# Half of the conditioning tiles of the second layer multiplied on POOL and summed by ACT instead of on DVE

## The chip, the cores and the metric

The kernel runs on one core of a Trainium2 chip. The metric is the device time of one execution in microseconds (us). One execution was also profiled, and all durations, waits and clocks below come from that one.

Engine names are those of the profile: PE is the matrix engine (PEld its weight loads), DVE the vector engine, ACT the scalar engine, POOL the GpSimd engine, SP the engine that only issues DMAs here. Each engine works through its own queue of instructions in order.

## What is computed

A trunk of two layers over 256 tokens of width 2048, all in float32. Each layer has a token mixer (an mLSTM in layer 0, softmax attention with forget gates, called FoX here, in layer 1) and a SwiGLU feed-forward network of inner width 5632. Both are wrapped in a normalisation that is modulated by six vectors, and these six vectors come from a conditioning vector `c`:

```
cs = jax.nn.silu(c)
for layer in range(DEPTH):
    mod = cs @ ada_w[layer] + ada_b[layer]
    sh1, sc1, g1, sh2, sc2, g2 = [m[:, None, :] for m in jnp.split(mod, 6, axis=-1)]
    h = rms_norm(x, norm_mix_w[layer]) * (1.0 + sc1) + sh1
    ...
    x = x + g1 * y
    h = rms_norm(x, norm_ffn_w[layer]) * (1.0 + sc2) + sh2
    x = x + g2 * swiglu(h, ffn_w_gate_up[layer], ffn_w_down[layer])
return rms_norm(x, final_norm_w)
```

The product `cs @ ada_w[layer]` is what the change is about: 2048 x 12288 weights per layer, for one row. It is a matrix-vector product, and nearly all of its cost is reading the matrix once.

## The kernel before, in words

**The large products.** Every large weight matrix is read in tiles of 4 x 128 rows by 512 columns (1 MB, `fetch`, L252 to L255) into a ring of five buffers, the pool `rawp`. To keep float32 accuracy on PE, each tile is split into a rounded high part and a rest (`split`, L257 to L265), two blocks of 128 rows at a time: ACT casts the high part `hi` (L263), and DVE subtracts it from the raw tile to get the low part `lo` (L264). Both go to a ring of four buffers (`splitp`). PE then makes three products for each block of 128 rows and each half of the tokens: L290, L291 and L292 in `mm_t`, where L291 uses `lo`. In `group_b`, used for the queries and keys of layer 1, the roles are exchanged and the products are L273 and L276. `group_a` and `group_b` loop over the rows of a matrix, four blocks of 128 at a time, and call `tick` after each.

**The conditioning.** The matrix `ada_w` is laid out so that one tile holds 128 output columns on the partitions and all 2048 inputs along the free axis. There are 96 such tiles of 1 MB per layer: six vectors (SH1, SC1, G1, SH2, SC2, G2) of 16 tiles. `ada_tile` (L191 to L198) takes a buffer from the same ring `rawp` as the weight tiles, issues the DMA on SP (L194), and lets DVE multiply the tile by the broadcast `cs` and sum along the free axis in one instruction (L195); the sum goes to one column of `acc`. After every fourth tile of a vector, `set_mods` (L177 to L189) turns four columns of `acc` into four columns of the finished vector, on DVE.

**What sets the order.** The conditioning tiles are background work. `want` puts tiles on a list, and `tick` calls `bg` with a rate: 0.75, 0.7, 0.8 and 0.5 tiles for each step of four row blocks in the four parts of the feed-forward network of layer 0, 0.66 in the FoX mixer, 0.3 in the last feed-forward network. The vectors SC1, SH1 and G1 of layer 1 are on the list from the middle of the feed-forward network of layer 0, SC2, SH2 and G2 of layer 1 from the start of the FoX mixer. Within these lists the tile framework's own scheduler orders each engine's queue, by the order of the program and by when it thinks an instruction is ready. The exception is the start of the kernel and the `bridge` (L527 to L590), the passage from one product to the next across a normalisation, where PE, DVE and ACT are listed by hand: a residual add on DVE (L429, L430), a sum of squares on ACT (L435), a reciprocal root (L454, L457), transposes on PE (L485), the affine part on ACT (L495) and on DVE (L497), the split (L510), and the first products of the next matrix (L552 to L556).

**POOL.** It holds little: constants at the start, a few memsets (L650, L633, L1202), and the DMAs of `grow` (L404, L412), which turn a finished gate vector into a row.

Of the kernel before, what the change touches and what calls it, by code (L numbers as in the profile page):

```python
# [12 lines left out]
AF = mybir.ActivationFunctionType  # L13
ALU = mybir.AluOpType
# [17 lines left out]
def kernel(  # L32
# [5 lines left out]
    nc = tc.nc  # L38
# [13 lines left out]
    def nm(s):  # L52
        n_name[0] += 1
        return f"{s}_{n_name[0]}"

    def slot(dt=F32):
        return slots.tile([P, 1024], dt, tag="slot", name=nm("slot"))
# [51 lines left out]
    acc = [const.tile([P, 96], F32, name=f"acc{i}") for i in range(2)]  # L109
# [15 lines left out]
    cs = const.tile([P, D], F32, name="cs")  # L125
# [41 lines left out]
    SH1, SC1, G1, SH2, SC2, G2 = range(6)  # L167
# [23 lines left out]
    def ada_tile(layer, vec, k):  # L191
        j = 16 * vec + k
        raw = rawp.tile([P, D], F32, tag="raw", name=nm("ada"))
        nc.sync.dma_start(raw, ada_w[layer, j])  # L194
        nc.vector.scalar_tensor_tensor(  # L195
            out=raw, in0=raw, scalar=1.0, in1=cs, op0=ALU.mult, op1=ALU.mult,
            accum_out=acc[layer][:, j : j + 1],
        )  # L198
# [17 lines left out]
    def bg(n):  # L216
        credit[0] += n
        while credit[0] >= 1.0 and background:
            credit[0] -= 1.0
            layer, v, k = background.pop(0)  # L220
            ada_tile(layer, v, k)
            if k % 4 == 3:
                set_mods(layer, v, k - 3, 4)
                done.add((layer, v, k // 4))
                if v in (G1, G2) and all((layer, v, q) in done for q in range(4)):
                    pending.append((layer, v))
        credit[0] = min(credit[0], 1.0)
# [516 lines left out]
    def early():  # L744
        for k in range(KT):
            for vec in (SC1, SH1):
                ada_tile(0, vec, k)
                if k == 0 and vec == SC1:
                    row_scale()
                set_mods(0, vec, k, 1)  # L750
                if vec == SC1:
                    yield
            if k < 4:
                norm_full(k)
            else:
                norm_tile(k, 0, SC1, SH1)
            at[0] = k + 1
            yield
# [17 lines left out]
    for k in range(4):  # L776
        upto(k + 1)
        for i in range(0, FIRST, 2):
            raw = slot()
# [209 lines left out]
    def keep_t(c0, bgn, scale=None, adv=1, layer_w=0):  # L989
        if layer_w == 0:  # L990
            i = COLS.index(c0)
            unit(i, start[i], KT, bgn)
            sp = SP[i]
            o = slot().rearrange("p (k t) -> p k t", t=T)

            def flip():
                for i in range(2):
                    nc.scalar.copy(o[:, 2 * i : 2 * i + 2, :], turned(sp, i))

            steps.append(flip)  # L1000
            return o
        o = slot().rearrange("p (k t) -> p k t", t=T)
        group_b(w, KT, c0, h_act, lambda m, ps: total(ps, o[:, m, :], scale), bgn, adv)
        return o
# [7 lines left out]
    for i in range(2):  # L1012
        q = keep_t(512 * i, LR[1 + i])
        k = keep_t(1024 + 512 * i, LR[1 + i])
# [193 lines left out]
    for i in range(4):  # L1208
# [5 lines left out]
        k = keep_t(D + 512 * i, FR, layer_w=1)  # L1214
# [123 lines left out]
```

## Time and profile before

| | us |
|---|---|
| median of two runs | 2300.57 (2300.23 to 2300.9) |
| the profiled execution, its own time | 2300.83 |
| its span, from first to last instruction | 2299.0 |
| ACT busy | 1122.8 |
| DMA queue q1, packets' time as a share of 16 engines | 74.3% |

The span is the time between the first and the last instruction of the core in the profiled execution; 1.8 us of the execution's own time lie outside it. An engine's busy time is the union of its instructions. In the view of groups, a row gives line, engine, operation, output and inputs with their shapes, the count, the busy time, the mean of one in ns, and after the second bar the idle time of that engine just before these instructions with what ended it. In the view of waits, a row gives who waited for whom, the total in us, how many times, and the longest. In the timeline, a row gives start, duration, engine, line and operation, with the idle time before it in brackets.

The layer-1 tiles that the change touches run in two stretches of the span: SC1, SH1 and G1 between 655 and 1003 us, SC2 and SH2 between 1151 and 1447 us. Between these two there is no conditioning work.

### The profile page before, as it was taken

The page shows a single profiled execution, that of the slowest core. Times are in us where ns is not written, and L with a number is a line of the kernel's source. Part 1 is how long each engine was busy: PE and PEld are TensorE (multiplying, and loading weights), DVE is VectorE, ACT ScalarE, POOL GpSimd, SP SyncE. Part 2 cuts the span into 40 slices and gives each one's busy share as a digit, 9 for nine tenths or more (in the row PEclk, how much of TensorE's full clock was granted, in tenths as well). Part 3 has the DMA queues.
Part 4 walks back from the last instruction along what each step waited for, and adds up shares of the span by engine and source line. Part 5 has one row for each costly group of instructions (what it writes and reads, how often), then busy time and mean ns, then how long its engine had stood idle before and what let it go on. Part 6 is the DMA issues. An engine that isn't in the chain of part 4 may idle for free.

```text
span 2299.0 us, 26543 instructions
## 1 busy us (share of the span) xinstructions
PE 2275.4 (99%) x10376; PEld 1861.0 (81%) x10376; DVE 1612.9 (70%) x1829; ACT 1122.8 (49%) x1488; POOL 15.6 (1%) x40
## 2 busy tenths in 40 slices
PE   8999999999999999999999999999999999999998
PEld 4777878888888888888878888888888888888886
DVE  5998788878887878865687777777655554544554
ACT  3778664555543344444555444455444433444443
POOL 0000000000000000000000000000000000000000
PEclk9999999999999999999999999999999999999999
DMA  9998989798989889985667878775766555555552
GB/s 348 364 368 320 355 313 362 271 345 325 331 331 336 323 337 337 342 293 188 215 243 285 300 259 288 255 275 186 250 241 222 191 191 198 189 187 195 193 196 105
DMA packets 89090, 623.92 MB, mean 271 GB/s; under 512 B 10034, under 2 KB 10482, under 8 KB 14596
## 3 DMA queue, kind: packets, MB, share of 16 engines
q1 hardware_dynamic: 87552, 617.79, 74.3%
q0 software_dynamic: 1264, 4.29, 0.5%
q8 instruction: 81, 1.33, 0.2%
q14 instruction: 45, 0.37, 0.0%
q10 hardware_dynamic: 148, 0.14, 0.0%
HBM read 620.05 MB, written 2.13 MB: 271 GB/s over the span
## 4 chain that ended last, share of the span: by engine, by line
PE 88%; DVE 6%; DMA 3%; ACT 2%; issue 1%; SPq 0%; ACTq 0%; DVEq 0%
PE mm L292 25%; PE mm L291 25%; PE mm L290 25%; PE mm L273 5%; DVE ada L195 3%; PE mm L276 2%; DVE lo L264 2%; DMA ada<-in_ada_w_dram 2%; PE aux L347 1%; ACT hi L263 1%; DMA raw<-in_w_in_dram 1%; DMA slot<-in_w_in_dram 1%; PE aux L945 0%; PE aux L485 0%; PE aux L1144 0%
## 5 line engine op out<-in xcount | busy, mean ns | idle before, releaser
L264 DVE TENSOR_TENSOR lo<-raw,hi 128x1024 fp32r<-128x1024 f32 x764 | 926.9, 1223 | 556.8 <-ACT hi L263 556.2
L263 ACT CAST hi<-raw 128x1024 fp32r<-128x1024 f32 x764 | 797.1, 1053 | 920.3 <-PE mm L292 816.9
L291 PE MATMUL mm<-lo,hT 128*128 128x512 f32 x1840 | 718.3, 390 | 5.3 <-DVE lo L264 5.3
L290 PE MATMUL mm<-hi,hT 128*128 128x512 f32 x1840 | 719.3, 393 | 0.0
L292 PE MATMUL mm<-hi,hT 128*128 128x512 f32 x1840 | 718.1, 390 | 0.0
L195 DVE SCALAR_TENSOR_TENSOR ada<-ada,cs 128x2048 f32<-128x2048 f32 x192 | 438.9, 2286 | 49.2 <-DMA ada<-in_ada_w_dram 49.2
L291 PEld LDWEIGHTS mm<-lo,hT 128*128 128x128 f32 x1840 | 345.7, 188 | 80.1 <-DVE lo L264 10.2
L292 PEld LDWEIGHTS mm<-hi,hT 128*128 128x128 f32 x1840 | 345.4, 188 | 72.7 <-issue 0.5
L290 PEld LDWEIGHTS mm<-hi,hT 128*128 128x128 f32 x1840 | 345.3, 188 | 70.9 <-ACT hi L263 0.5
L290 PE MATMUL mm<-hi,slot 128*128 128x512 f32 x960 | 375.1, 391 | 0.2 <-ACT slot L978 0.2
L291 PE MATMUL mm<-lo,slot 128*128 128x512 f32 x960 | 374.4, 390 | 0.0
L292 PE MATMUL mm<-hi,slot 128*128 128x512 f32 x960 | 374.4, 391 | 0.0
L290 PEld LDWEIGHTS mm<-hi,slot 128*128 128x128 f32 x960 | 180.3, 188 | 37.7 <-ACT slot L978 0.8
L292 PEld LDWEIGHTS mm<-hi,slot 128*128 128x128 f32 x960 | 180.2, 188 | 37.6 <-issue 0.7
L291 PEld LDWEIGHTS mm<-lo,slot 128*128 128x128 f32 x960 | 180.2, 188 | 37.0
L273 PE MATMUL mm<-hT,hi 128*128 128x512 f32 x512 | 181.7, 402 | 0.6 <-DVE slot L359 0.6
L276 PE MATMUL mm<-hT,lo 128*128 128x256 f32 x512 | 138.3, 280 | 0.0
L273 PEld LDWEIGHTS mm<-hT,hi 128*128 128x128 f32 x512 | 94.4, 188 | 20.5 <-DVE slot L359 0.9
L276 PEld LDWEIGHTS mm<-hT,lo 128*128 128x128 f32 x512 | 96.6, 189 | 3.0
L800 ACT ACTIVATE slot<-mm 128x512 f32<-128x512 f32 x78 | 45.0, 593 | 33.9 <-PE mm L292 31.1
L435 ACT ACTIVATE t<-X 128x512 f32<-128x512 f32 x32 | 20.2, 631 | 39.2 <-DVE X L430 39.2
L1085 ACT ACTIVATE slot<-mm 128x512 f32<-128x512 f32 x44 | 25.4, 598 | 15.0 <-PE mm L292 13.8
(207 smaller groups left out, 980.5 us busy)
## 6 DMA issues: line engine op xcount, KB each, us to landing
ada<-in_ada_w_dram SPq DMA_DIRECT2D x192, 1024.0 KB, 6.5
raw<-in_gate_up_dram SPq DMA_DIRECT2D x176, 1024.0 KB, 4.9
raw<-in_down_dram SPq DMA_DIRECT2D x88, 1024.0 KB, 4.9
raw<-in_fox_in_dram SPq DMA_DIRECT2D x48, 1024.0 KB, 5.0
raw<-in_w_in_dram SPq DMA_DIRECT2D x44, 1024.0 KB, 7.3
raw<-in_w_out_dram SPq DMA_DIRECT2D x16, 1024.0 KB, 5.8
raw<-in_fox_out_dram SPq DMA_DIRECT2D x16, 1024.0 KB, 4.9
slot<-in_w_in_dram SPq DMA_DIRECT2D x16, 256.0 KB, 12.1
```

The lines of the kernel that those rows point to most:

```text
L195: nc.vector.scalar_tensor_tensor(out=raw, in0=raw, scalar=1.0, in1=cs, op0=ALU.mult, op1=ALU.mult, accum_out=acc[layer][:, j : j + 1],)
L263: nc.scalar.copy(hi, raw[:, j : j + 2, :])
L264: nc.vector.tensor_tensor(lo, raw[:, j : j + 2, :], hi.bitcast(F32), op=ALU.subtract)
L273: nc.tensor.matmul(ps, hi, rhs, start=first, stop=last, skip_group_check=True)
L276: nc.tensor.matmul(ps[:, T:], lo, rhs[:, :T], start=False, stop=False, skip_group_check=True)
L290: nc.tensor.matmul(ps, a, hi, start=first, stop=False, skip_group_check=True)
L291: nc.tensor.matmul(ps, a, lo, start=False, stop=False, skip_group_check=True)
L292: nc.tensor.matmul(ps, b, hi, start=False, stop=last, skip_group_check=True)
L347: nc.tensor.transpose(ps[:, j * T + t * P : j * T + (t + 1) * P], src[:, t, (2 * i + j) * P : (2 * i + j + 1) * P], ident,)
L435: nc.scalar.activation(t512(), X[:, t, 512 * i : 512 * (i + 1)], AF.Square, accum_out=self.ss[:, t, i : i + 1],)
L800: nc.scalar.activation(SP[i][:, t, :], banks[t], func)
L1085: nc.scalar.activation(sg[:, t, :], banks[t], AF.Silu)
```

## The change

Of the tiles of layer 1, those with an even index `k` in all vectors but G2 leave DVE. That is 5 vectors x 8 tiles, 40 of the 192 tiles. For each, POOL multiplies the tile by `cs` in place, and ACT then passes over the product with a copy that sums along the free axis into the same column of `acc`. The other tiles, and what follows from `acc`, stay as they are.

```diff
@@ -192,6 +192,10 @@
         j = 16 * vec + k
         raw = rawp.tile([P, D], F32, tag="raw", name=nm("ada"))
         nc.sync.dma_start(raw, ada_w[layer, j])
+        if layer == 1 and vec != G2 and k % 2 == 0:
+            nc.gpsimd.tensor_tensor(raw, raw, cs, op=ALU.mult)
+            nc.scalar.activation(raw, raw, AF.Copy, accum_out=acc[layer][:, j : j + 1])
+            return
         nc.vector.scalar_tensor_tensor(
             out=raw, in0=raw, scalar=1.0, in1=cs, op0=ALU.mult, op1=ALU.mult,
             accum_out=acc[layer][:, j : j + 1],
```

## The prediction, made before the change was run

> **What bounds the kernel now.** I read the page first, for the engines' shares of the span.
>
> ```profile
> span 2299.0 us, 26543 instructions
> ...
> PE 2275.4 (99%) x10376; PEld 1861.0 (81%) x10376; DVE 1612.9 (70%) x1829; ACT 1122.8 (49%) x1488; POOL 15.6 (1%) x40
> ```
>
> PE is busy for all but 23.6 us. DVE, which the change relieves, is busy 70%. A share says little about the stretches that are touched, so the next view is the windows, cut where the touched tiles run: all engines first, then line L195 alone (instructions in brackets; each tile is two, the multiply and the read of its sum).
>
> ```profile
> 655.00:1003.00 348.00, 347.52 (x1554) 287.47 (x1553) 278.25 (x273) 143.34 (x147) 1.58 (x3) 1.00 0.90 335
> ...
> 1151.00:1447.00 296.00, 294.43 (x1575) 249.20 (x1574) 227.42 (x318) 145.29 (x239) 2.23 (x3) 1.00 0.77 276
> ```
>
> ```profile
> 655.00:1003.00 348.00, 110.11 (x96) 1.00 0.90 335
> ...
> 1151.00:1447.00 296.00, 73.51 (x64) 1.00 0.77 276
> ```
>
> The columns are PE, PEld, DVE, ACT, POOL, clock, DMA share and GB/s. In the first stretch 48 tiles run, 24 of which move; in the second 32, of which 16 move. PE is idle 0.48 us in the first and 1.57 us in the second, at full clock. DVE has 70 us and 69 us to spare, ACT more than half, POOL is empty. What PE waited for between 655 and 1447 us is the third view:
>
> ```profile
> PE mm L556 <- DVE hT L510: 0.9, 1, 0.9
> PE mm L273 <- DVE slot L359: 0.6, 1, 0.6
> PE aux L347 <- DVE slot L1088: 0.5, 1, 0.5
> ```
>
> Three waits, 2.0 us in all, none for a weight tile. So the stretches are bound by PE, and work taken off DVE can return at most 2.0 us. The question is what the new route can do to PE's supply.
>
> **How far ahead of PE the supply is.** The timeline of ACT, DVE and SP around 945 us shows the beat.
>
> ```profile
> 945.74 1.06 ACT L263 CAST hi<-raw 128x1024 fp32r<-128x1024 f32 x1 [1.67 <-PE mm L292]
> 948.46 1.05 ACT L263 CAST hi<-raw 128x1024 fp32r<-128x1024 f32 x1 [1.66 <-PE mm L292]
> 951.18 1.06 ACT L263 CAST hi<-raw 128x1024 fp32r<-128x1024 f32 x1 [1.67 <-PE mm L292]
> ...
> 956.62 1.06 ACT L263 CAST hi<-raw 128x1024 fp32r<-128x1024 f32 x1 [1.67 <-PE mm L292]
> ```
>
> ```profile
> 945.25 2.28 DVE L195 SCALAR_TENSOR_TENSOR ada<-ada,cs 128x2048 f32<-128x2048 f32 x1
> 947.46 0.08 DVE L195 DVE_READ_ACCUMULATOR ada<-ada,cs 128x1 f32 x1
> 947.46 1.22 DVE L264 TENSOR_TENSOR lo<-raw,hi 128x1024 fp32r<-128x1024 f32 x1
> ...
> 956.13 2.28 DVE L195 SCALAR_TENSOR_TENSOR ada<-ada,cs 128x2048 f32<-128x2048 f32 x1
> ...
> 958.66 1.37 DVE L1088 TENSOR_TENSOR slot<-mm,slot 128x512 f32<-128x512 f32 x2 [0.24 <-PE mm L292]
> 959.95 2.35 DVE L264 TENSOR_TENSOR lo<-raw,hi 128x1024 fp32r<-128x1024 f32 x2
> ```
>
> ```profile
> 939.41 0.33 SPq L254 DMA_DIRECT2D raw<-in_gate_up_dram  x1
> ```
>
> A cast starts each time PE gives back a buffer of the split ring, every 2.72 us. The ring has four buffers, so the pair cast at 945.74 is used three beats later, at 945.74 + 3 x 2.72 = 953.9. Its `lo` ends at 947.46 + 1.22 = 948.7, 5.2 us ahead. At 956.62 a conditioning tile and two other operations stood in front of `lo`, which ended near 961.2; its use comes at 964.8, and 3.6 us were still left. **The margin is 5.2 us, 3.6 us in a busy spot.** Counting fetches and casts (two casts a fetch), the fetch issued at 939.41 is cast at 951.18; with 4.9 us to land, as the page has it for this tensor, it lay ready for 6.9 us.
>
> **The change part by part.** The rows for the durations, from the groups by form (whole execution), and two of the groups in the first stretch:
>
> ```profile
> L800 ACT ACTIVATE slot<-mm 128x512 f32<-128x512 f32 x78 | 45.0, 593 | 33.9 <-PE mm L292 31.1 <-PE mm L786 1.3
> L195 DVE DVE_READ_ACCUMULATOR ada<-ada,cs 128x1 f32 x192 | 15.8, 82 | 0.0
> L435 ACT ACTIVATION_READ_ACCUMULATOR t<-X 128x1 f32 x32 | 6.0, 186 | 0.0
> L650 POOL MEMSET slot<- 128x1024 f32 x4 | 3.8, 958 | 229.2 <-PE mm L553 142.2 <-PE aux L786 48.1 <-DVE t L382 38.9
> ```
>
> ```profile
> L263 ACT CAST hi<-raw 128x1024 fp32r<-128x1024 f32 x126 | 132.9, 1055 | 198.9 <-PE mm L292 195.6 <-DVE ada L195 1.7 <-DVE lo L264 1.7
> ...
> L195 DVE SCALAR_TENSOR_TENSOR ada<-ada,cs 128x2048 f32<-128x2048 f32 x48 | 109.7, 2286 | 8.1 <-DMA ada<-in_ada_w_dram 8.1
> ```
>
> *Removed from DVE:* 40 x (2.286 + 0.082) = 40 x 2.37 = 94.7 us. PE is the bound, so its worth is between 0 and -2.0 us; I take 0, since the three waits hang on other lines.
>
> *Added on ACT:* 40 passes over 128x2048. 512 elements take 0.593 and 1024 take 1.055, so 1024 more cost 0.92 and the pass 1.98; with 0.19 for reading the sum, 2.16 us. 40 x 2.16 = 86 us. In the stretches ACT goes from 143.3 to 195 of 348 us, and from 145.3 to 180 of 296: room enough. Hidden behind the 1.67 us in which ACT waits at every beat.
>
> *Added on POOL:* 40 multiplies of 128x2048. The trace has no two-input operation on POOL. The nearest row is the memset: 0.958 us for 1024 elements that are written and not read, so 1.92 us for 2048 is a bound from below; if two reads and the write took three such passes one after the other, 5.75 us is a bound from above. I take two passes, 3.8 us. 40 x 3.8 = 153 us on an empty engine. The Trainium skill (GPSIMD Engine Reference, 3.1 Elementwise) gives 4497 ns for a two-input float32 operation of 2048 elements on GpSimd and 2293 ns on the vector engine; the second agrees with the 2286 ns here, and by the first the POOL sum would be 180 us, still hidden.
>
> *The buffer is held longer:* 3.8 + 2.16 in place of 2.37, some 3.6 us more, for 40 buffers of a ring of five. SP issues in order and waits for these buffers already:
>
> ```profile
> SPq L254 <- DVE ada L195: 102.3, 34, 5.1
> ```
>
> (between 650 and 1010 us). A fetch that is 3.6 us late still lies ready 6.9 - 3.6 = 3.3 us before its cast. I cost this at 0; without that cover it would be up to 3.6 us for each moved tile.
>
> *The new wait, and what is queued behind it:* ACT's pass waits for POOL, and the casts behind it on ACT's queue wait with it; then `lo` on DVE; then PE. If ACT reaches its pass when POOL starts, it is held 3.8 + 2.16 = 6.0 us; 1.67 of these were idle anyway, so the cast is 4.3 us late against a margin of 5.2. That holds in the usual spot and misses by 0.7 us in the busy one (3.6). If one tile in eight falls there, 5 x 0.7 = 3.5 us. Bounds: 0, and 40 x 0.7 = 28 us.
>
> *One tile lies in the bridge.* The first tile of the second stretch (SC2, k = 0, one that moves) runs on DVE at 1151.86, just ahead of the hand-ordered chain:
>
> ```profile
> 1151.86 2.29 DVE L195 SCALAR_TENSOR_TENSOR ada<-ada,cs 128x2048 f32<-128x2048 f32 x1 [2.23 <-DMA ada<-in_ada_w_dram]
> ...
> 1154.08 0.69 DVE L429 TENSOR_TENSOR t<-mm,slot 128x512 f32<-128x512 f32 x1
> 1154.80 0.69 DVE L430 TENSOR_TENSOR X<-X,t 128x512 f32<-128x512 f32 x1
> ```
>
> ```profile
> 1155.53 0.63 ACT L435 ACTIVATE t<-X 128x512 f32<-128x512 f32 x1 [7.15 <-DVE X L430]
> ...
> 1158.11 1.50 ACT L495 ACTIVATE hT<-aux,mods 128x128 fp32r<-128x128 f32 x4 [1.53 <-PE aux L485]
> ```
>
> With POOL from 1151.9 to 1155.7, ACT's pass would fall at 1155.7 to 1157.8, between L435 and L495, a chain that PE already waited for by 0.9 us (L556). It delays L435 or L454 by up to 2.16 us. Against that DVE may come to L429 up to 2.3 us earlier. Bounds -0.9 and +2.2; I take +1.5.
>
> Sum: 2300.8 (the profiled execution's own time, 0.3 above the median of the runs) + 0 + 3.5 + 1.5 = **2306 us**, which is no change within 2% (46 us, about what a measurement of this kernel can tell from no change). Own range: 2299 to 2330.
>
> **The rivals.**
>
> *A: POOL and DVE keep each other waiting.* Both would read the memory at once, and if two-input operations exclude each other, each moved tile blocks DVE while POOL multiplies. In the first stretch DVE's time becomes 278.25 - 24 x 2.37 + 24 x h. With h = 3.8 that is 313 of 348 us; it decides from h = (348 - 278.25 + 56.9) / 24 = 5.3 us. At the upper bound, 5.75, it is 359, 11 us over; the second stretch stays under (227.4 - 37.9 + 92 = 281.5 of 296). With the 5 us above: 2317 us. For it speaks that L264 and L195, most of DVE's time, have two inputs in the same memory; against it, that no row shows DVE and POOL at work together. The Trainium skill (SBUF — State Buffer, Who interferes with whom) says just this: a vector instruction with two SBUF inputs and a GpSimd instruction that reads SBUF exclude each other for a whole instruction. No run here shows it yet; with the skill's 4.5 us as h it would be 329 of 348, below the point.
>
> *B: ACT stands in front of POOL, and PE runs dry (the slower side).* If POOL starts late, after L195 and L264 on DVE (2.29 + 1.22 = 3.5 us), ACT's hold grows to 3.5 + 3.8 + 2.16 = 9.5 us; less the idle 1.67, the cast is 7.8 late, PE stands 7.8 - 5.2 = 2.6 us. It decides once the hold exceeds 5.2 + 1.67 = 6.9 us. With every second tile hit: 20 x 2.6 = 52 us, 2353 us. For it: a strict queue with the casts behind the pass. Against it: the scheduler puts the pass where it thinks that POOL has finished, and DVE's own waits for these tiles' DMAs were short in the first stretch (8.1 us for 48).
>
> *C: only relief.* The pass always falls into ACT's idle time, POOL is quick, and the three waits go: 2300.8 - 2.0 = 2299 us. For it: POOL and ACT have the room. Against it: the waits are not at moved tiles.
>
> **How the numbers follow.** The forecast gets 0.58, A 0.17, B 0.14, C 0.11. The time is the forecast's, 2306. The range goes from C's 2299, less 1 us for the runs' own spread, 2298, to 2340, between A and B; it leaves out most of B. A gain of over 2% would need 46 us where PE idles 23.6 in all: 0.01. Slower by over 2% is B with the tail of A: 0.14. The rest, 0.85, is within.
>
> **What would show it.** Right: L195 on DVE at 152 instead of 192, POOL busy some 150 us more, ACT some 86 us more, DVE down by 95, and PE's busy time unchanged; PE's new waits for L263 and L264 between 655 and 1447 us under 10 us. POOL's mean duration between 1.9 and 5.75 us. A shows as L264 or L195 lengthened or late while POOL works, with DVE near full in the first stretch. B shows as casts on ACT that wait for POOL's line or follow a pass late, and PE waits of 2 us and more. The prediction is wrong if PE's idle time in the two stretches grows by more than 30 us, or if the time falls below 2298.

## The result, and the profile after

The changed kernel takes 2366.36 us (median of two runs, 2364.32 to 2368.4) against 2300.57 before. The ratio is 1.0286, with an interval of 1.0242 to 1.033: slower by 66 us. The forecast was 2306 within 2298 to 2340, so it missed, on the slow side. The profiled execution took 2368.4 us, its span is 67.6 us longer than before.

The page of the changed kernel first (from here on, lines of the code stand four higher than before: L196 is POOL's multiply, L197 ACT's pass, L199 DVE's conditioning tile, L267 the cast of `hi`, L268 `lo`, L294 to L296 the products; in the experiments they shift by some lines again).

```profile
span 2366.6 us, 26636 instructions
...
PE 2298.4 (97%) x10376; PEld 1864.7 (79%) x10376; DVE 1621.4 (69%) x1749; ACT 1188.5 (50%) x1568; POOL 208.8 (9%) x80
...
L268 DVE TENSOR_TENSOR lo<-raw,hi 128x1024 fp32r<-128x1024 f32 x764 | 1006.9, 1333 | 601.3 <-ACT hi L267 600.9
...
L199 DVE SCALAR_TENSOR_TENSOR ada<-ada,cs 128x2048 f32<-128x2048 f32 x152 | 347.3, 2285 | 22.3 <-DMA ada<-in_ada_w_dram 22.3
L196 POOL TENSOR_TENSOR ada<-ada,cs 128x2048 f32<-128x2048 f32 x40 | 193.3, 4833 | 939.7 <-DMA ada<-in_ada_w_dram 771.0
...
L197 ACT ACTIVATE ada<-ada 128x2048 f32<-128x2048 f32 x40 | 76.7, 1917 | 204.1 <-POOL ada L196 204.1
```

Three things are to be seen. PE is idle for 2366.6 - 2298.4 = 68.2 us, where it was 23.6. DVE has lost 40 tiles and is busier than before, 1621.4 against 1612.9 us, chiefly because `lo` takes 1333 ns on average where it took 1223, 80 us in all. And ACT stood idle 204.1 us ahead of its 40 passes, all of it waiting for POOL: 5.1 us a pass.

The windows of the same trace show where PE idles; their bounds follow the moved tiles, which now run later.

```profile
655.00:1027.00 372.00, 352.96 (x1532) 283.02 (x1531) 288.62 (x222) 179.03 (x191) 113.67 (x27) 1.00 0.81 306
1178.00:1510.00 332.00, 308.04 (x1600) 254.94 (x1598) 218.23 (x284) 171.45 (x271) 78.76 (x19) 0.98 0.66 242
```

PE idles 19.0 us in the first stretch and 24.0 us in the second, where it idled 0.48 and 1.57. No engine but PE is near full in either. PE's waits name who was late, first from 640 to 1045 us, then from 1150 to 1600 us:

```profile
PE mm L295 <- DVE lo L268: 11.8, 19, 2.1
PE aux L351 <- DVE slot L1092: 5.4, 3, 2.8
PE mm L294 <- ACT hi L267: 1.5, 4, 0.5
...
PE aux L1180 <- DVE slot L369: 9.0, 2, 5.1
PE mm L280 <- DVE lo L268: 8.8, 14, 1.7
PE aux L489 <- DVE slot L478: 4.1, 2, 2.6
```

The split weight tiles (`hi` and `lo`), for which PE never waited in these stretches before, come late in both; in the second so do the operands of the small products of the FoX mixer (L1180, two long waits).

To compare kernels stretch by stretch, the 776 casts of `hi` serve as milestones, since they come in the same order in every version. Cast 208 starts at 663.69 us before and 661.33 after, cast 344 at 1040.28 and 1066.70: over the first stretch the change loses 28.8 us. Between the stretches (casts 344 to 384) it loses nothing. From cast 384 (1141.88 and 1168.31) to cast 520 (1573.23 and 1640.55) it loses 40.9 us. All of the loss lies in these two stretches (28.8 + 40.9 = 69.7 us; ahead of cast 208 the changed kernel is 2.4 us early).

**The first stretch, in the timeline of ACT, POOL and DVE at 784 us.**

```profile
784.32 1.05 ACT L267 CAST hi<-raw 128x1024 fp32r<-128x1024 f32 x1 [1.34 <-PE mm L296]
793.03 1.92 ACT L197 ACTIVATE ada<-ada 128x2048 f32<-128x2048 f32 x1 [7.67 <-POOL ada L196]
...
794.94 3.88 ACT L267 CAST hi<-raw 128x1024 fp32r<-128x1024 f32 x4
```

```profile
788.40 4.60 POOL L196 TENSOR_TENSOR ada<-ada,cs 128x2048 f32<-128x2048 f32 x1 [11.24 <-DVE lo L268]
```

```profile
796.00 2.36 DVE L268 TENSOR_TENSOR lo<-raw,hi 128x1024 fp32r<-128x1024 f32 x2 [7.78 <-ACT hi L267]
```

ACT reached the pass at 785.4, three microseconds before POOL began to multiply, and stood until 793.03. Four casts were queued behind the pass and then ran back to back. DVE stood for 7.78 us with nothing to subtract from. This is rival B's picture.

**The second stretch, on POOL and DVE at 1348 us.**

```profile
1348.01 5.44 POOL L196 TENSOR_TENSOR ada<-ada,cs 128x2048 f32<-128x2048 f32 x1 [14.96 <-ACT t L359]
```

```profile
1347.76 1.23 DVE L268 TENSOR_TENSOR lo<-raw,hi 128x1024 fp32r<-128x1024 f32 x1
1348.90 0.42 DVE L363 SCALAR_TENSOR_TENSOR slot<-mm,t 128x256 f32<-128x256 f32 x1
1349.35 5.17 DVE L268 TENSOR_TENSOR lo<-raw,hi 128x1024 fp32r<-128x1024 f32 x1
```

A `lo` that takes 1.23 us at 1347.76 takes 5.17 us at 1349.35 and ends 1 us after POOL's multiply does. L363, which has one operand in PSUM, took its usual time meanwhile. This is rival A's lock. It shows by shape in the groups of DVE from 640 to 1600 us, for the residual add in its two halves:

```profile
L434 DVE TENSOR_TENSOR X<-X,t 128x512 f32<-128x512 f32 x20 | 22.6, 1144 | 0.2
L433 DVE TENSOR_TENSOR t<-mm,slot 128x512 f32<-128x512 f32 x20 | 13.3, 684 | 3.1 <-PE mm L296 3.1
```

Both are the same size. L433, with one operand in PSUM, keeps the 0.69 us that it had before. L434, with both in SBUF, had 0.69 and now takes 1.144 on average: three of the 20 met a multiply and were held, one of them up to 5.02 us.

**The clock.** A part of the loss is PE at half speed. The granted clock was 0.5 for 20.5 us in all, in four pieces (3.41 us from 697.1, 6.83 from 1376.4, 3.41 from 1444.7, 6.83 from 1523.2), each beginning within an idle time of PE. One of the four in PE's timeline and in the windows:

```profile
1378.94 1.22 PE L1180 MATMUL aux<-slot,slot 128*128 128x256 f32 x2 [5.05 <-DVE slot L369]
```

```profile
1376.00:1384.00 8.00, 5.06 (x15) 4.24 (x16) 6.92 (x11) 3.45 (x7) 0.00 (x0) 0.57 0.69 237
```

The clock column stands at 0.57. PE was busy for 16.0 of the 20.5 us; at half speed that is some 8 us of work. So of 67.6 us, 44.6 are PE's idle time (23.6 to 68.2) and 23.0 are PE being busy longer (2275.4 to 2298.4), some 8 of these by the clock. The other 15 lie beside the idle times. Set product by product against the trace before, those just ahead of an idle time or just behind one take 14.7 us longer in all, and there are 82 idle times of over 0.02 us where there were 27. (The ends of PE's products are modelled in the profile, so the split between idle and busy is rough.)

### The profile page after: what moved, and what is told of

Same layout as the page of the kernel before. It is cut to its first block, busy times and chain, and to the rows that moved or that the text cites. A ratio compares the mean times of both kernels' runs of the same rounds, so it can differ in the third digit from the quotient of the medians.

```text
span 2366.6 us, 26636 instructions
## 1 busy us (share of the span) xinstructions
PE 2298.4 (97%) x10376; PEld 1864.7 (79%) x10376; DVE 1621.4 (69%) x1749; ACT 1188.5 (50%) x1568; POOL 208.8 (9%) x80
## 5 line engine op out<-in xcount | busy, mean ns | idle before, releaser
L268 DVE TENSOR_TENSOR lo<-raw,hi 128x1024 fp32r<-128x1024 f32 x764 | 1006.9, 1333 | 601.3 <-ACT hi L267 600.9
L267 ACT CAST hi<-raw 128x1024 fp32r<-128x1024 f32 x764 | 790.3, 1052 | 718.7 <-PE mm L296 668.5
L294 PE MATMUL mm<-hi,hT 128*128 128x512 f32 x1840 | 719.7, 393 | 0.1
L296 PE MATMUL mm<-hi,hT 128*128 128x512 f32 x1840 | 718.6, 391 | 0.0
L296 PEld LDWEIGHTS mm<-hi,hT 128*128 128x128 f32 x1840 | 345.7, 188 | 72.1 <-issue 0.5
L294 PEld LDWEIGHTS mm<-hi,hT 128*128 128x128 f32 x1840 | 345.6, 188 | 71.7 <-ACT hi L267 0.9
L294 PE MATMUL mm<-hi,slot 128*128 128x512 f32 x960 | 376.8, 392 | 1.6 <-ACT hi L267 1.5
L296 PE MATMUL mm<-hi,slot 128*128 128x512 f32 x960 | 375.2, 392 | 0.0
L199 DVE SCALAR_TENSOR_TENSOR ada<-ada,cs 128x2048 f32<-128x2048 f32 x152 | 347.3, 2285 | 22.3 <-DMA ada<-in_ada_w_dram 22.3
L196 POOL TENSOR_TENSOR ada<-ada,cs 128x2048 f32<-128x2048 f32 x40 | 193.3, 4833 | 939.7 <-DMA ada<-in_ada_w_dram 771.0
L294 PEld LDWEIGHTS mm<-hi,slot 128*128 128x128 f32 x960 | 180.8, 188 | 41.2 <-ACT hi L267 3.4
L296 PEld LDWEIGHTS mm<-hi,slot 128*128 128x128 f32 x960 | 180.8, 188 | 37.4 <-issue 0.7
L197 ACT ACTIVATE ada<-ada 128x2048 f32<-128x2048 f32 x40 | 76.7, 1917 | 204.1 <-POOL ada L196 204.1
L804 ACT ACTIVATE slot<-mm 128x512 f32<-128x512 f32 x78 | 45.0, 593 | 34.3 <-PE mm L296 31.6
```

The lines of the kernel that those rows point to most:

```text
L196: nc.gpsimd.tensor_tensor(raw, raw, cs, op=ALU.mult)
L197: nc.scalar.activation(raw, raw, AF.Copy, accum_out=acc[layer][:, j : j + 1])
L199: nc.vector.scalar_tensor_tensor(out=raw, in0=raw, scalar=1.0, in1=cs, op0=ALU.mult, op1=ALU.mult, accum_out=acc[layer][:, j : j + 1],)
L267: nc.scalar.copy(hi, raw[:, j : j + 2, :])
L268: nc.vector.tensor_tensor(lo, raw[:, j : j + 2, :], hi.bitcast(F32), op=ALU.subtract)
L294: nc.tensor.matmul(ps, a, hi, start=first, stop=False, skip_group_check=True)
```

## The experiments

**Two theories** went into them. *The queue (B, Theory Q in the expectations):* the pass on ACT stands in front of POOL's end and the casts behind it starve PE. *The lock (A, Theory L):* POOL's multiply shuts out DVE's operations with two inputs in SBUF. Both are seen in the trace; the question is which costs the time. Each experiment starts from the changed kernel. Ratios are against the kernel before on the same chip (2297.75 to 2298.7 us). Losses by stretch come from the one profiled execution of each kernel.

**POOL alone.** The pass on ACT is left out (the 40 columns of `acc` are zeroed once, at the start); POOL multiplies as in the change.

```diff
-            nc.scalar.activation(raw, raw, AF.Copy, accum_out=acc[layer][:, j : j + 1])
```

> POOL multiplies the 40 tiles as in the change, but ACT's pass is left out, so that the 40 sums are missing (their columns of acc are zeroed once). Nothing on ACT waits for POOL. Theory Q (the pass stands on ACT's queue in front of POOL's end, and the casts behind it come late): the loss is gone but for lo that POOL holds up, 2300 to 2311 us. Theory L (POOL's multiply and DVE's two-input operations shut each other out, and lo comes late): most of the 66 us stays, 2340 to 2366 us, and L264's operations that overlap a POOL multiply last up to 5.6 us.

2338.79 us, 1.0179 [1.0164, 1.0194]. The first stretch loses 4.6 us, the second 36.1. From its page, its line L268 and PE's waits from 1150 to 1620 us:

```profile
L197 POOL TENSOR_TENSOR ada<-ada,cs 128x2048 f32<-128x2048 f32 x40 | 198.0, 4950 | 901.5 <-DMA ada<-in_ada_w_dram 373.0
```

```profile
L268 DVE TENSOR_TENSOR lo<-raw,hi x764: 1185/1224/5644, 54.9 to 2323.0; 128x1024 fp32r<-128x1024 f32 x191
```

```profile
PE mm L280 <- DVE lo L268: 10.1, 19, 2.2
PE aux L1180 <- DVE slot L369: 8.4, 2, 5.6
```

(The second row gives least, median and longest in ns.) The longest `lo` is as long as in the change, with nothing on ACT to wait for. In the first stretch 24 operations of DVE are held (they take over 0.2 us more than in the kernel before), for 79.7 us in all, in the second 16, for 57.2. So the lock by itself costs the second stretch most of what the change loses there, and the first next to nothing, though more time is held there.

**Writes only.** POOL writes the tile (1.8 + 1.8 + 0.75 us in three memsets, 4.4 us) and reads nothing; the pass stays.

```diff
-            nc.gpsimd.tensor_tensor(raw, raw, cs, op=ALU.mult)
+            nc.gpsimd.memset(raw, 0.0)
+            nc.gpsimd.memset(raw, 1.0)
+            nc.gpsimd.memset(raw[:, :768], 0.0)
```

> In place of the multiply POOL writes the tile with constants, 2048 + 2048 + 768 elements in three memsets, which by the row of 0.958 us for 1024 take 4.6 us, as long as the multiply (4.6); it reads nothing. ACT's pass waits for it as in the change; the 40 sums are those of constants. Theory Q: the loss stays, 2345 to 2366 us, with waits of ACT for POOL of about 200 us in total. Theory L: without reads on POOL no DVE operation is held, the loss is gone, 2300 to 2311 us. If both are at work, in between.

2301.84 us, 1.0016 [1.0006, 1.0025]. No `lo` is longer than 1.23 us. That takes the lock away, but it was no clean test of the queue: the scheduler now placed the passes later, and ACT hardly waited.

```profile
L199 ACT ACTIVATE ada<-ada 128x2048 f32<-128x2048 f32 x40 | 76.7, 1916 | 17.0 <-POOL ada L198 16.9
```

**The pass behind.** Nothing is left out; each pass is put on ACT's queue behind the last cast that the program has before it, later than where the change has it.

```diff
-            nc.scalar.activation(raw, raw, AF.Copy, accum_out=acc[layer][:, j : j + 1])
+            with tc.issue_after(cast[0].ins):
+                nc.scalar.activation(raw, raw, AF.Copy, accum_out=acc[layer][:, j : j + 1])
...
-        nc.scalar.copy(hi, raw[:, j : j + 2, :])
+        cast[0] = nc.scalar.copy(hi, raw[:, j : j + 2, :])
```

> The change, with ACT's pass put behind the last cast that the program has before it (an order on ACT's queue, no wait). The pass comes one to four casts later, when POOL should have finished; POOL's multiply and the work on every engine stay. Theory Q: ACT's waits for POOL fall from 204 us to under 60, and the time to 2300 to 2315 us. Theory L: lo is held as before, 2340 to 2360 us.

2319.69 us, 1.0095 [1.0072, 1.0119]: 4.7 us lost in the first stretch, 15.2 in the second. ACT's wait for POOL and the line of `lo`:

```profile
ACT ada L198 <- POOL ada L196: 23.7, 12, 3.6
```

```profile
L270 DVE TENSOR_TENSOR lo<-raw,hi x764: 1189/1224/5645, 49.6 to 2297.0; 128x1024 fp32r<-128x1024 f32 x191
```

The wait fell from 204.1 to 23.7 us, the lock stayed. In the first stretch this takes the loss away but for the 4.7 us that POOL alone costs as well; in the second a part remains that the lock explains: none of the 23.7 us of waiting lies there, and the writes before, with passes but no lock, lost 4.5.

**The multiply in four pieces**, the pass as in the change.

```diff
-            nc.gpsimd.tensor_tensor(raw, raw, cs, op=ALU.mult)
+            for i in range(4):
+                c = slice(512 * i, 512 * (i + 1))
+                nc.gpsimd.tensor_tensor(raw[:, c], raw[:, c], cs[:, c], op=ALU.mult)
```

> The change, with POOL's multiply cut into four of 512 columns, so that DVE is held at most about 1.2 us at a time; ACT's pass stays where it was and waits for the fourth. Theory Q: the same loss or a little more, 2355 to 2385 us. Theory L: DVE comes in between the pieces, 2300 to 2320 us.

2399.87 us, 1.0441 [1.0426, 1.0457]; 54.5 and 48.5 us lost. From the page and the waits:

```profile
L198 POOL TENSOR_TENSOR ada<-ada,cs 128x512 f32<-128x512 f32 x160 | 253.5, 1614 | 916.8 <-DMA ada<-in_ada_w_dram 768.3
```

```profile
ACT ada L199 <- POOL ada L198: 252.8, 39, 8.8
```

The longest `lo` fell from 5.67 to 2.352 us, so DVE gets in between the pieces; but POOL now needs 4 x 1.614 = 6.5 us a tile, ACT waits 252.8 us, and the kernel is slower. Shorter locks don't help while ACT's queue waits for POOL.

**Pieces, and the pass behind**: the two edits above together.

```diff
+            for i in range(4):
+                c = slice(512 * i, 512 * (i + 1))
+                nc.gpsimd.tensor_tensor(raw[:, c], raw[:, c], cs[:, c], op=ALU.mult)
+            with tc.issue_after(cast[0].ins):
+                nc.scalar.activation(raw, raw, AF.Copy, accum_out=acc[layer][:, j : j + 1])
```

> Both remedies at once: POOL's multiply in four of 512 columns, and ACT's pass behind the last cast that the program has before it. Nothing is left out. If what was left with the pass behind alone (21 us over before, 15 of them in the FoX stretch) is DVE held for a whole multiply, it goes: 2299 to 2308 us. If it is the waiting of ACT that is left, it stays or grows, since the four pieces took 6.5 us a tile when they were tried alone: 2315 to 2330 us.

2320.18 us, 1.009 [1.0072, 1.0108]; 19.2 and 5.9 us lost. Beside the pass behind alone (4.7 and 15.2), the second stretch loses less with the short locks. That this is their doing is likely but not shown: it rests on one trace of each, and the runs of the pass behind alone spread from 2314.35 to 2327.12 us. The first loses, because POOL's four pieces take 4 x 1850 ns = 7.4 us a tile and ACT waits for POOL again, 78.0 us in that stretch.

**Writes only, with the pass ahead.** As the second experiment, but each pass is put ahead of the next casts by hand, where the change has it, so that the queue can be tested without the lock. For this the background tile is emitted between a fetch and its casts.

```diff
+            ahead[0] = nc.scalar.activation(
+                raw, raw, AF.Copy, accum_out=acc[layer][:, j : j + 1]
+            )
...
+        if ahead[0] is not None:
+            with tc.issue_after(ahead[0].ins):
+                nc.scalar.copy(hi, raw[:, j : j + 2, :])
+            ahead[0] = None
...
+        if rate_now[0] is not None and background and background[0][0] == 1 and background[0][1] != G2:
+            bg(rate_now[0])
+            rate_now[0] = 0.0
```

> POOL writes constants for 4.4 us a tile and reads nothing, as before, but ACT's pass now stands where the change has it on ACT's queue, ahead of the casts (in the first stretch at the same casts as in the change, in the FoX stretch up to two later). The 40 sums are those of constants. Theory Q alone (the wait of ACT needs no help from the lock): ACT waits for POOL 100 us and more, and the first stretch loses 15 to 28 us as in the change (28.8), so 2315 to 2335 us. If the loss of the first stretch needs the lock as well: under 8 us there, 2300 to 2310 us.

2301.59 us, 1.0013 [1.0003, 1.0022]; 1.6 us lost in each stretch. ACT's group from 640 to 1010 us:

```profile
L199 ACT ACTIVATE ada<-ada 128x2048 f32<-128x2048 f32 x24 | 46.0, 1918 | 46.2 <-POOL ada L198 46.2
```

A wait of 46.2 / 24 = 1.9 us and a pass of 2.1 hold ACT for 4.0 us on average, and no hold is over 6.8 us: hidden. The wait of 100 us and more for which this run was made did not come about, so it does not yet say what a wait as long as that of the change costs.

**The same order, with the multiply**, nothing left out.

```diff
-            nc.gpsimd.memset(raw, 0.0)
-            nc.gpsimd.memset(raw, 1.0)
-            nc.gpsimd.memset(raw[:, :768], 0.0)
+            nc.gpsimd.tensor_tensor(raw, raw, cs, op=ALU.mult)
```

> The run with constants and the pass ahead, with POOL's multiply put back; ACT's pass stands at the same casts, and nothing is left out. The two differ in what POOL executes alone. Theory L (the lock is needed for the loss): 2350 to 2375 us, as the change, against 2302 with constants. Theory Q (the wait of ACT alone): no higher than 2310 us, since the order on ACT is the one that cost nothing there.

2377.55 us, 1.0349 [1.0329, 1.0369]; 34.8 and 38.8 us lost, ACT waits 202.4 us. With the same order by hand, the multiply in place of the writes brings the change's loss back. It brings the lock and the long wait together, so this run does not part the two.

**Every fourth tile**, 20 in place of 40.

```diff
-        if layer == 1 and vec != G2 and k % 2 == 0:
+        if layer == 1 and vec != G2 and k % 4 == 0:
```

> The change for every fourth tile in place of every second: 20 moved tiles. If each moved tile costs by itself (1.65 us a tile in the change), half of the loss stays: 2325 to 2340 us. If the loss comes from moved tiles that follow before the supply has recovered, much more than half goes: 2300 to 2318 us.

2330.71 us, 1.0141 [1.0125, 1.0157]; 9.5 and 19.6 us. Half of the tiles cost (2330.71 - 2298.7) / 20 = 1.6 us each, all of them 66 / 40 = 1.65. So 20 tiles are not free, and in all the cost goes with their number. By stretch it does so less well: 9.5 / 12 = 0.8 us a tile in the first, where it was 28.8 / 24 = 1.2, and 2.5 in the second, where it was 2.6.

**One input on POOL.** Can POOL be made to read less?

```diff
-            nc.gpsimd.tensor_tensor(raw, raw, cs, op=ALU.mult)
+            nc.gpsimd.tensor_scalar(raw, raw, 1.0, None, op0=ALU.mult)
```

> POOL multiplies the tile by 1.0 in place, so it reads one input from memory in place of two; ACT's pass stands at the same casts as in the change, and the 40 sums are those of the plain weights. If any read by POOL shuts out DVE's two-input operations, L264 is held here too until POOL has finished, and the loss goes with POOL's duration: with some 2 to 3 us a tile, 2302 to 2325 us. If only two reads do: no L264 over 1.4 us, and 2298 to 2306 us.

2389.96 us, 1.0394 [1.0378, 1.041]; 43.3 and 47.8 us. Its page, and its line of `lo`:

```profile
L196 POOL TENSOR_SCALAR ada<-ada 128x2048 f32<-128x2048 f32 x40 | 230.1, 5752 | 924.2 <-DMA ada<-in_ada_w_dram 424.2
```

```profile
L268 DVE TENSOR_TENSOR lo<-raw,hi x764: 1187/1224/4699, 50.2 to 2368.8; 128x1024 fp32r<-128x1024 f32 x191
```

With one input POOL is slower (5752 ns, not 4833, and far from the 2 to 3 us expected), and `lo` is still held and takes up to 4.699 us.

**A longer write, with the pass ahead.** Two more memsets of the whole tile: POOL takes 8.0 us a tile, ACT waits as long as in the change, and nothing is locked.

```diff
             nc.gpsimd.memset(raw, 1.0)
+            nc.gpsimd.memset(raw, 0.0)
+            nc.gpsimd.memset(raw, 1.0)
             nc.gpsimd.memset(raw[:, :768], 0.0)
```

> The run with constants and the pass ahead, with two more memsets of 2048 elements, so that POOL writes for 8.0 us a tile and still reads nothing. ACT reaches its pass as early as in the change and has to wait about as long for POOL as there (204 us in total), with no operation of DVE held. The 40 sums are those of constants. If waiting on ACT alone starves PE: 2320 to 2350 us, with PE waits behind casts. If the wait does harm only together with the lock: under 2306 us, although ACT waits 150 us and more.

2342.48 us, 1.0195 [1.0176, 1.0214]; 39.4 us lost in the first stretch, 2.9 in the second. ACT's group and PE's waits from 640 to 1050 us, and the line of `lo`:

```profile
L201 ACT ACTIVATE ada<-ada 128x2048 f32<-128x2048 f32 x24 | 46.0, 1917 | 122.7 <-POOL ada L200 122.7
```

```profile
PE mm L310 <- ACT hi L277: 14.8, 8, 3.5
PE mm L311 <- DVE lo L281: 6.4, 10, 1.9
```

```profile
L281 DVE TENSOR_TENSOR lo<-raw,hi x764: 1189/1224/1229, 49.7 to 2320.0; 128x1024 fp32r<-128x1024 f32 x191
```

No `lo` is longer than 1.229 us, and yet the first stretch loses more than in the change, at the same wait: the change has 123.1 us there. (PE's waits are 21 us of the loss; the clock was at one half for 27.3 us of this run, which is some 12 more.) Nor do late weight tiles explain it: POOL holds its buffers longer here, but the least time that a weight tile lay ready before its cast was 6.4 us, more than the 4.2 us of the kernel before.

```profile
L197 ACT ACTIVATE ada<-ada 128x2048 f32<-128x2048 f32 x24 | 46.0, 1918 | 123.1 <-POOL ada L196 123.1
```

**All together.** Loss in us against the kernel before, by casts 208 to 344 and 384 to 520; ACT's waits for POOL ahead of the passes of these stretches (24 and 16, or half of that). The losses and waits are those of one execution each; the runs of one kernel lie up to 13 us apart, so smaller differences between two rows are not shown.

| kernel | median, us | first stretch | second stretch | ACT waits for POOL | longest `lo` |
|---|---|---|---|---|---|
| the change | 2366.36 | 28.8 | 40.9 | 123.1 / 81.0 | 5.67 |
| POOL alone | 2338.79 | 4.6 | 36.1 | 0 / 0 | 5.64 |
| pass behind | 2319.69 | 4.7 | 15.2 | 23.7 / 0 | 5.65 |
| pieces | 2399.87 | 54.5 | 48.5 | 158.7 / 94.0 | 2.35 |
| pieces, pass behind | 2320.18 | 19.2 | 5.9 | 78.0 / 4.9 | 2.40 |
| order by hand | 2377.55 | 34.8 | 38.8 | 125.5 / 76.9 | 5.64 |
| every fourth tile | 2330.71 | 9.5 | 19.6 | 44.2 / 33.2 | 5.63 |
| one input | 2389.96 | 43.3 | 47.8 | 130.6 / 94.5 | 4.70 |
| writes only | 2301.84 | 1.1 | 4.5 | 10.4 / 6.6 | 1.23 |
| writes, pass ahead | 2301.59 | 1.6 | 1.6 | 46.2 / 6.1 | 1.23 |
| longer writes, pass ahead | 2342.48 | 39.4 | 2.9 | 122.7 / 27.4 | 1.23 |

In the first stretch the loss follows ACT's wait and not the lock: 1.6 us at 46.2 of waiting and 39.4 at 122.7, both without any lock, and 4.6 without a wait under the full lock. In the second, locks without waiting cost 36.1 and 15.2 us, and no kernel without the lock loses more than 4.5. What stays open: why the lock costs 36.1 us in one order of DVE's queue and 15.2 in another (it holds 16 operations for 57.2 us in the first case and 15 for 41.3 in the second, which alone does not give a factor of two); and what ACT's wait alone costs in the second stretch, where the kernel made for it waits only 27.4 us. A ring of more buffers, which might hide the wait, was not tried. No version that was run beats the kernel before.

## Why the prediction was wrong

**PE bounds, and relief of DVE is worth nothing: right.** With writes only, DVE's busy time is 1529.5 us, 83 below before, and the time stays at 2301.84.

**ACT's pass, 2.16 us: right.** It took 1.917 + 0.183 = 2.10. ACT's busy time still rose by 65.7 us only, not 86, because instructions that follow each other closely overlap, casts for one: the four at 794.94 take 3.88 us, one takes 1.05.

**The bridge, +1.5: the right number by another path.** Casts 384 to 392 took 34.70 us before and 36.12 after, +1.4. But the pass did not fall between L435 and L495 (now L439 and L499). It stood ahead of L439, from 1174.8 us, waited 6.89 us for POOL and let L439 start at 1183.61, while the multiply stretched the residual add L434 from 0.69 to 2.29 us. That the sum is the one forecast is in part luck.

**POOL's multiply, 3.8 us: too short by a fifth.** It takes 4.613 in the median and 4.833 on average, since DVE's operations hold POOL up as well. It lies within the bounds of 1.92 and 5.75, and the choice of two memset passes inside them was the weak point. The figure that the prediction took from the Trainium skill (GPSIMD Engine Reference, 3.1 Elementwise), 4497 ns, agrees with the shortest multiply of this trace, 4.579 us.

**The failed step: "The new wait, and what is queued behind it".** It put the hold of ACT at 6.0 us for every tile, below the 6.9 us from which rival B decides, and so its whole cost at 3.5 us. Its picture was right for the first stretch: on average ACT reaches the pass 5.13 - 4.83 = 0.3 us before POOL starts. But with the measured terms the hold is 0.3 + 4.83 + 2.10 = 7.2 us on average, and it varies. Of the 24 holds of that stretch (wait and pass, in ACT's timeline) the shortest is 3.8 us and the longest 9.8, and 13 lie beyond 6.9. So "one tile in eight" falls as well: more than half of the tiles overran the margin of even the usual spot. In all, 39 of the 40 passes waited for POOL, as the waits of ACT and DVE from 655 to 1510 us show.

```profile
ACT ada L197 <- POOL ada L196: 204.1, 39, 7.7
DVE lo L268 <- ACT hi L267: 198.3, 108, 9.1
```

Set against the busy margin of 3.6 us, the prediction's own formula gives 7.2 - 1.67 - 3.6 = 1.9 us a tile; the first stretch lost 28.8 / 24 = 1.2. The mean of the hold does not decide: pieces with the pass behind lost 19.2 us at a mean of 5.35. What the holds overrun does better. Summed over the first stretch, what lies beyond 6.9 us in each hold is a floor that the loss exceeds in every run, by 1.1 to 17.4 us:

| kernel | holds beyond 6.9 us | their excess, us | loss, us |
|---|---|---|---|
| writes only; writes, pass ahead; pass behind | 0 of 24 | 0 | 1.1; 1.6; 4.7 |
| every fourth tile | 4 of 12 | 4.5 | 9.5 |
| pieces, pass behind | 5 of 24 | 8.1 | 19.2 |
| longer writes, pass ahead | 10 of 24 | 22.0 | 39.4 |
| order by hand | 14 of 24 | 24.6 | 34.8 |
| the change | 13 of 24 | 24.9 | 28.8 |
| one input | 15 of 24 | 33.3 | 43.3 |
| pieces | 20 of 24 | 48.4 | 54.5 |

The same step failed a second time in the second stretch, where the larger part of the loss lies (40.9 us). Its margins were read at one place of the first stretch and taken for all 40 tiles; the second had no term but the bridge. There the runs show the lock at work: 36.1 us without any pass on ACT. The prediction's own sign of being wrong, PE's idle time in the two stretches up by more than 30 us, came true: it rose by 41.

**The buffer held longer, costed at 0: not the direct cause.** SP now waits for ACT's passes, here from 655 to 1010 us.

```profile
SPq L258 <- ACT ada L197: 72.2, 13, 9.0
```

The least time that a weight tile lay ready before its cast fell from 4.2 us or more to 1.05 us (between 900 and 1010 us). No cast waited for a tile there, so this cover held.

**Rival B, 2353 us, had the right mechanism for the first stretch.** What was argued against it, "the scheduler puts the pass where it thinks that POOL has finished", did not help: four casts stood behind the pass at 793.03. For the memsets, that it did place right by itself, ACT waited 17.0 us in all. It is likely, though only argued from this, that it takes the multiply to be shorter than it is.

**Rival A, 2317 us, had the right lock and the wrong place.** It looked for a DVE that becomes full, from 5.3 us a tile. DVE was never full (288.62 of 372 us, 218.23 of 332). Single operations were held for up to 4.4 us instead (5.67 in place of 1.22), and that hit the FoX stretch, where PE waits for small products that DVE hands over (L1180 after L369), not the first. The two then add up: at 1368 us POOL multiplies, ACT stands 6.13 us before its pass, and the step of the mixer behind it (L359) leaves DVE idle for 7.37 and PE for 5.05 us.

```profile
1373.18 1.91 ACT L197 ACTIVATE ada<-ada 128x2048 f32<-128x2048 f32 x1 [6.13 <-POOL ada L196]
...
1375.09 0.91 ACT L359 ACTIVATE t<-mm 128x256 f32<-128x256 f32 x3
```

```profile
1375.49 1.09 DVE L361 TENSOR_TENSOR slot<-mm,t 128x256 f32<-128x256 f32 x3 [7.37 <-ACT t L359]
```

The runs agree with what the prediction named from the Trainium skill (SBUF — State Buffer, Who interferes with whom): two inputs in SBUF on DVE against a read on POOL exclude each other, the residual add with one operand in PSUM does not suffer, and POOL's memsets hold nothing. They also show one held operation that has a single tile from SBUF, a multiply by a column of numbers: L1170 took 4.365 us in place of 0.28.

**The clock was in no term.** Idle times of a few microseconds on PE brought half speed, some 8 us of the 66.

## What to carry to other kernels

An operation moved to an empty engine can still cost time on the engine that takes up its result, if work queued in order stands behind it there. Work out how long the consumer's queue is held (the wait for the producer and the pass), for single cases and not only in the mean, set that against the margin of what is queued behind it, in each stretch, and be wary of a verdict of "no change" that rests on 0.9 us between a guessed duration and the point from which it tips: the guess must then be carried at its upper bound. With POOL and DVE the price of a read on POOL is not only POOL's time but a stalled operation of DVE as well (26 for the 40 multiplies of the change), and that hurts where a short operation of DVE, not its total, is what PE waits for.

## What the runs showed of the hardware

- POOL's multiply by a constant with one input takes longer than its multiply of two tensors of the same size (5752 against 4833 ns on average, 5359 against 4579 at least), and still shuts out DVE. It lets DVE go earlier: the longest `lo` was 4.699 us beside it, 5.673 beside the two-input form.
- Four multiplies of 512 columns take 6.5 to 7.4 us where one of 2048 takes 4.8. The shortest piece took 1.268 us, four of them 5.1; the rest goes with DVE getting its turn in between.
- The Trainium skill (TensorE: Matmul & The Clock Gate, Why this matters for your kernels) warns of PE idle for more than some 3 us. Here the clock also halved for 3.41 us within an idle time of 2.75 us on PE (it ended at 697.8 us), and within the second of two short ones of 1.64 and 0.76 us (they ended at 1443.7 and 1445.0), while 2.56 us (1210.8) and 2.15 us (951.3) brought nothing. The four half-speed pieces of the changed kernel start whole multiples of 3.413 us apart (199, 20 and 23 times). Where an idle time falls on this grid may thus decide; that is not shown.
